# A 1 KB strip at the end of the last store, spread unevenly over the transfer engines

One Trainium2 chip, one core. The metric is the time of one execution in device microseconds; each kernel was run several times, and all runs compared here are of the fast state (a single run counts as of unknown state and is marked).

## The reference

The kernel turns 32 x 3 images of 256 x 256 float32 by 180 degrees. Seen flat, each image is reversed.

```python
def reference(x):                       # x: (32, 3, 256, 256) float32
    return np.rot90(x, k=2, axes=(-2, -1)).astype(np.float32)
```

## The kernel before

The 96 images are taken in three groups of 32. One image lies on four partitions, a quarter of it (E = 16384 elements, 64 KB) on each, so one group fills a tile of 128 partitions. VectorE reverses each row inside the tile in pieces; the store writes the four quarters of an image in reverse order. All transfers are issued by the sync engine.

```python
    G = 32
    E = L // 4                       # 16384 elements, 64 KB per partition
    ...
    def load(t, g, lo=0, hi=E):
        nc.sync.dma_start(out=t[:, lo:hi], in_=x4[g][:, lo:hi])

    def store(t, g):
        nc.sync.dma_start(out=o4[g][:, ::-1, :], in_=t[:, :])
    ...
    load(A, 0, 0, N)                 # N = E // 32
    load(A, 0, N, E)
    load(Bt, 1)
    load(Ct, 2)
    for g, t in enumerate((A, Bt, Ct)):
        inside(t)                    # 12 VectorE copies reverse each row
        store(t, g)
```

## Time and profile before

| | before |
|---|---|
| time, median of 3 runs (range) | 123.1 us (123.06 to 123.44) |
| span of the profiled run | 121.1 us |
| packet time, share of 16 engines | 97.4% |
| VectorE busy | 36% |

The time is that of a whole execution; the span runs from the first to the last instruction of one profiled execution. The page's main lines stand in the prediction below. One more, from the timeline of before (start, length, engine, line, operation), shows when the sync engine has nothing more to issue:

```profile
76.33 1.23 DVE L53 COPY Ct<-T 128x2048 f32<-128x2048 f32 x1
77.59 0.54 SPq L59 DMA_DIRECT2D out_dram<-Ct  x1
```

The last copy ends at 77.6 us and the last store is issued at once. The other 43.5 us are transfers draining, then the close of the program.

Three kinds of record in the trace are finer than the page, and the argument rests on them: each transfer engine's **packets** (start, length, size), the **landings** (the times at which a transfer's completion mark of one engine arrives at its semaphore, 16 for a transfer over 16 engines) and the sync engine's **waits** at the end. Numbers in ns below come from these records.

### The profile page before, as it was taken

The numbers are of one execution on the slowest core, as the hardware profiler recorded it, in microseconds if no ns is written. First come the engines' busy times: TensorE is split into PE (matmuls) and PEld (weight loads), VectorE is DVE, ScalarE is ACT, GpSimd is POOL, SyncE is SP. The second block draws the span as 40 slices with busy tenths as digits, with TensorE's granted clock in tenths as the row PEclk, the third lists the DMA queues.
The fourth block names the chain that finished last, engine by engine and source line by source line (L and its number), as shares of the span: only waits on it lengthen the run. The fifth ranks groups of instructions, "written<-read, shape, count | busy, mean of one in ns | idle before, by whom it ended". The sixth has DMA issues, their size and how long they took to land.

```text
span 121.1 us, 94 instructions
## 1 busy us (share of the span) xinstructions
DVE 44.2 (36%) x36; POOL 0.2 (0%) x4
## 2 busy tenths in 40 slices
DVE  0000000599994199998039999600000000000000
POOL 0000000000000000000000000000000000000000
DMA  9977987897799879978989977997799779977980
GB/s 359 399 336 336 650 356 336 346 693 346 346 411 628 346 346 476 563 346 346 346 346 476 563 346 346 563 476 346 346 584 455 346 346 606 433 346 346 671 368 0
DMA packets 1008, 50.33 MB, mean 416 GB/s; under 512 B 112, under 2 KB 112, under 8 KB 240
## 3 DMA queue, kind: packets, MB, share of 16 engines
q1 hardware_dynamic: 1008, 50.33, 97.4%
HBM read 25.17 MB, written 25.17 MB: 416 GB/s over the span
## 4 chain that ended last, share of the span: by engine, by line
DMA 33%; DVE 25%; another core or an unknown queue 4%; issue 1%; SPq 1%; DVEq 0%
DMA Bt<-in_x_dram 33%; DVE T L53 8%; DVE Ct L53 8%; DVE Bt L53 8%; SPq L56 1%; DVEq L53 0%
## 5 line engine op out<-in xcount | busy, mean ns | idle before, releaser
L53 DVE COPY T<-A 128x2048 f32<-128x2048 f32 x4 | 4.9, 1227 | 22.7 <-DMA A<-in_x_dram 22.6
L53 DVE COPY T<-Ct 128x2048 f32<-128x2048 f32 x4 | 4.9, 1227 | 5.4 <-DMA Ct<-in_x_dram 5.3
L53 DVE COPY T<-Bt 128x2048 f32<-128x2048 f32 x4 | 4.9, 1227 | 4.4 <-DMA Bt<-in_x_dram 4.3
L53 DVE COPY Bt<-T 128x2048 f32<-128x2048 f32 x4 | 4.9, 1227 | 0.1
L53 DVE COPY A<-T 128x2048 f32<-128x2048 f32 x4 | 4.9, 1227 | 0.1
L53 DVE COPY Ct<-Ct 128x2048 f32<-128x2048 f32 x4 | 4.9, 1227 | 0.1
L53 DVE COPY Bt<-Bt 128x2048 f32<-128x2048 f32 x4 | 4.9, 1227 | 0.1
L53 DVE COPY A<-A 128x2048 f32<-128x2048 f32 x4 | 4.9, 1227 | 0.1
L53 DVE COPY Ct<-T 128x2048 f32<-128x2048 f32 x4 | 4.9, 1227 | 0.1
L89 POOL MEMSET const-bfloat16-1.0<- 128x1 bf16 x1 | 0.1, 101 | 0.0
L89 POOL MEMSET const-uint8-127<- 128x1 uint8 x1 | 0.1, 101 | 0.0
L89 POOL MEMSET const-float32-0.0<- 128x1 f32 x1 | 0.1, 98 | 0.2 <-issue 0.2
L89 POOL MEMSET const-float32-1.0<- 128x1 f32 x1 | 0.1, 98 | 0.0
## 6 DMA issues: line engine op xcount, KB each, us to landing
A<-in_x_dram SPq DMA_DIRECT2D x1, 7936.0 KB, 21.4
A<-in_x_dram SPq DMA_DIRECT2D x1, 256.0 KB, 2.8
Bt<-in_x_dram SPq DMA_DIRECT2D x1, 40.3
Ct<-in_x_dram SPq DMA_DIRECT2D x1, 60.3
out_dram<-A SPq DMA_DIRECT2D x1, 43.9
out_dram<-Bt SPq DMA_DIRECT2D x1, 43.8
out_dram<-Ct SPq DMA_DIRECT2D x1, 42.7
```

The lines of the kernel that those rows point to most:

```text
L53: tc.keep_in_program_order(nc.vector.tensor_copy(out=dst, in_=src))
L56: nc.sync.dma_start(out=t[:, lo:hi], in_=x4[g][:, lo:hi])
L89: nc = _bacc.Bacc("TRN2", target_bir_lowering=False, num_devices=1)
```

## The change

The intent is to even out the ends of the sixteen transfer engines, which do not finish the last store together. The store is cut 1 KB short on every row, and the strip that is left goes out in four transfers whose shapes put more rows on low-numbered engines and none on 14 and 15.

```diff
+    M = E // 64
-    def store(t, g):
-        nc.sync.dma_start(out=o4[g][:, ::-1, :], in_=t[:, :])
+    def store(t, g, lo=0, hi=E, i=0, j=G):
+        nc.sync.dma_start(out=o4[g][i:j, ::-1, lo:hi], in_=t[4 * i:4 * j, lo:hi])
 ...
-    for g, t in enumerate((A, Bt, Ct)):
-        inside(t)
-        store(t, g)
+    inside(A)
+    store(A, 0)
+    inside(Bt)
+    store(Bt, 1)
+    inside(Ct)
+    store(Ct, 2, 0, E - M)
+    store(Ct, 2, E - M, E, 0, 14)
+    store(Ct, 2, E - M, E, 14, 16)
+    store(Ct, 2, E - M, E, 16, 24)
+    store(Ct, 2, E - M, E, 24, 32)
```

## The prediction

> **What bounds the kernel now.** I read the head of the page first, to see whether an engine or the transfers fill the span.
>
> ```profile
> span 121.1 us, 94 instructions
> DVE 44.2 (36%) x36; POOL 0.2 (0%) x4
> ...
> DMA packets 1008, 50.33 MB, mean 416 GB/s; under 512 B 112, under 2 KB 112, under 8 KB 240
> ## 3 DMA queue, kind: packets, MB, share of 16 engines
> q1 hardware_dynamic: 1008, 50.33, 97.4%
> ```
>
> VectorE works for 36% of the span; packets fill 97.4% of what sixteen transfer engines have. So this is a kernel of transfers, and only two things shorten it: less packet time on the engine that ends last, or a shorter tail behind it. The 112 packets under 512 B are no data: 7 transfers times 16 engines, one 4-byte semaphore packet each.
>
> The chain of waits stops at 77.6 us, when the last store is issued, so I take the end from the sync queue's own waits and from the list of issues.
>
> ```profile
> SPq L100 <- DMA out_dram<-Bt: 19.3, 1, 19.3
> SPq L100 <- DMA out_dram<-Ct: 19.3, 1, 19.3
> SPq L100 <- DMA out_dram<-A: 3.5, 1, 3.5
> ...
> out_dram<-A SPq DMA_DIRECT2D x1, 43.9
> out_dram<-Bt SPq DMA_DIRECT2D x1, 43.8
> out_dram<-Ct SPq DMA_DIRECT2D x1, 42.7
> ```
>
> At the end the sync engine waits for store A, then 19.3 us more for Bt's, then 19.3 us more for Ct's. Each store takes some 43 us to land although its own packets need 19.3 us, because it queues behind older transfers. From 77.6 us the rings are therefore always full, and whatever the sync engine issues in the microseconds after that is hidden. Windows show how abruptly it ends (columns: stretch and length, VectorE busy, GpSimd busy, clock, DMA share, GB/s):
>
> ```profile
> 112.00:119.40 7.40, 0.00 (x0) 0.00 (x0) 1.00 0.98 425
> 119.40:120.00 0.60, 0.00 (x0) 0.00 (x0) 1.00 0.01 0
> 120.00:121.10 1.10, 0.00 (x0) 0.00 (x0) 1.00 0.00 0
> ```
>
> No data packet starts after 119.4 us; behind it are the semaphore packets, the landing and the close.
>
> The packet records in the trace give the rest, in us from the start of the span. The sixteen engines end their last data packet between 119.431 and 119.970: sorted, at 0, 75, 118, 172, 186, 223, 312, 313, 314, 328, 347, 398, 419, 429, 440 and 539 ns after the first. The landings on the last store's semaphore lie between 119.783 and 120.313, the same pattern some 0.34 us later. In the instruction records the sync engine's last wait starts at 120.330, the next instruction at 120.397, and the span ends at 121.103: 0.79 us from the last landing, spent on barriers. The strip goes for the uneven end. If all engines ended at their mean, offset 288 ns, the gain would be 539 - 288 = 251 ns, 0.2% of 123.1. That is the most that any such balancing can bring.
>
> **What the Trainium skill says.** "DMA: Bandwidth & Descriptors", section "Why a DMA increments its semaphore by 16 and not by 1": the number of engines is the largest k up to 16 that divides the slowest dimension of both sides, and these are the lowest-numbered k. Groups of 14, 2, 8 and 8 with four rows each therefore go to engines 0 to 13, 0 and 1, 0 to 7 and 0 to 7, four rows per engine, as the title says. The trace before agrees for k = 16 (16 landings per transfer); its records do not name the engine, so it has nothing on which engine ends when. Section "Queues, rings and completion order": each engine consumes its ring in order. The trace agrees: packets follow each other without a gap, across transfers too, a 4-byte packet costing 6 ns between them. Section "Why small descriptors are slow (HBM only)": a fixed overhead of about 3 cycles per packet. In the trace 2048 B packets start every 80 ns and 65536 B packets every 2414 ns, so a packet costs 4.7 ns plus 0.03676 ns per byte: a small overhead indeed. Section "Latency and other measured facts": engines 7 and 15 are usually the slower ones. No record here can show it.
>
> **The change part by part.** All loads, all copies, the stores of A and Bt: unchanged. The order of instructions shows one thing only, four more issues on the sync engine behind the last store.
>
> Issues: four at about 0.54 us (what the last store's issue took) are 2.2 us, from 78.1 to 80.3, some 39 us before they are needed. Path cost 0.
>
> Base of the last store: 8 packets per engine shrink from 65536 to 64512 B, 8 x 1024 x 0.03676 = 301 ns less on each engine.
>
> Strip: a 1 KB packet should cost 4.7 + 37.6 = 42.4 ns, an estimate from the two sizes above. Engines 0 and 1: 16 x 42.4 = 678. Engines 2 to 7: 12 x 42.4 = 509. Engines 8 to 13: 4 x 42.4 = 170. Engines 14 and 15: none. Semaphore packets at 6 ns add 24, 18, 6 and 0. Against before, each kind of engine ends by
>
> - 0 and 1: -301 + 678 + 24 = +401 ns
> - 2 to 7: -301 + 509 + 18 = +226 ns
> - 8 to 13: -301 + 170 + 6 = -125 ns
> - 14 and 15: -301 ns
>
> Now lay these on the sixteen offsets. The kindest assignment is that engines end in order of their number, as the change supposes. Then 0 and 1 come to 401 and 476, 2 to 7 to 344, 398, 412, 449, 538 and 539, the others to at most 304. The latest is 539, just what it was: the strip moves 701 ns between the ends of the row, where only 539 ns were to be evened out, and engines 6 and 7 become the last. Gain 0. If finishing order has nothing to do with the number, drawing the assignment at random 20,000 times makes the latest 257 ns later on average, 401 at worst.
>
> The close: the built program waits at its end for pairs of semaphores. Before, the last store's was in the last wait, and the others had long been met. After, eight semaphores serve eleven transfers, and the fourth strip's sits in the second of the four waits, the base's and third strip's in the third, the first two strips' in the last. Engines 0 to 7, which end last, carry the fourth strip; so its landing releases the second wait, and two more waits have to be stepped through. From the records a satisfied wait takes 67 ns to the next instruction (120.330 to 120.397): 2 x 67 = +134 ns.
>
> Sum: 0 + 134 = +0.13 us with order by number, 257 + 134 = +0.39 us without order. The first moments of the trace speak for a mixture. The first packets of the sixteen engines start one after the other within 0.52 us, about the 0.43 us which that issue takes, so order by number exists at the very start; but the earliest had first packets of about 600 ns and later ones of 81 ns, which scrambles it. I give order 45%, no order 55%: 0.45 x 0.13 + 0.55 x 0.39 = +0.27. I add nothing for the measurement: 123.10 + 0.27 = 123.37, and I say 123.4.
>
> **The rivals.** First, the change does what it is meant to: late engines relieved, up to 0.25 us gained, less 0.13 for the waits, so 122.9 to 123.0. It needs an ordered end with a wider spread than this one execution shows, or 1 KB packets cheaper than 42 ns; neither is in the records. Second, small writes cost more than their bytes: before has no packet of 1 KB and none under 64 KB on the store side, and the 80 ns come from reads of HBM. Were 1 KB writes to cost 80 ns, the engines with 16 rows would lose 16 x 38 = 0.6 us more and those with 12 rows 0.45: 123.8 to 124.2. Against it speaks that ring order lets the next packet start without waiting for a write's receipt; nothing shows it for writes of this size. Third, all is hidden or drowned: a change of 0.1 us against runs of before that lie between 123.06 and 123.44. That would read 123.1 to 123.2, and is what order by number nearly gives. Fourth, a wait before issue: the strips reuse the loads' semaphores, and a missing completion could hold back an issue. The built program has no wait on them, as all four loads were awaited before.
>
> **Range and chances.** The low end is order by number with a quick run, 122.95; the high end is no order, with strip packets at some 60 ns (12 to 16 rows x 18 ns = 0.2 to 0.3 us): 123.5 + 0.3 = 123.8. A change of 2% is 2.5 us; the strip's whole packet time on the most loaded engine is 0.7 us, so it would take an effect that I have no trace of. Faster by over 2%: the bound of 0.25 us excludes it but for an error of mine, 0.005. Slower: 0.015. Within: 0.98.
>
> **What would show it.** Packets: 128 of 64512 B about 2377 ns apart, 128 of 1024 B about 42 ns apart, 14 + 2 + 8 + 8 = 32 more semaphore packets: 1008 + 128 + 32 = 1168 in all. The page: DMA share still about 97%, VectorE unchanged, four more issues that end near 80.3 us. The last two waits of the sync engine some 67 ns apart and both behind the last landing. Engines that carry 12 or 16 rows should be the last; the spread of the last data packets should be as large as before or larger. Wrong would be: 1 KB packets at 60 ns or more (second rival), a spread well under 0.5 us (first rival), or a gap before the strip's packets, which would mean that the new transfers are not ready in the ring in time.

## The result

The changed kernel took 123.13 us (median of 6 runs, 123.06 to 123.57), before 123.06 (6 runs, 122.72 to 123.44). The ratio is 1.0013, with a 95% interval of 0.999 to 1.0037. Ratios here are the mean time of one kernel's runs over that of the other's of the same rounds, so not quite the ratio of the medians. So: the same within 2%, inside the predicted range of 122.95 to 123.8, and 0.27 us below the predicted 123.4. A second measurement (the run "again" below) gave 1.0012, 1.0000 to 1.0025. The first interval contains 1 and the second touches it, so the times by themselves do not settle that the change costs anything; what follows on its parts comes from single traces.

From the head of the page of the changed kernel:

```profile
span 121.4 us, 98 instructions
DVE 44.2 (36%) x36; POOL 0.2 (0%) x4
...
DMA packets 1168, 50.33 MB, mean 415 GB/s; under 512 B 144, under 2 KB 272, under 8 KB 400
...
q1 hardware_dynamic: 1168, 50.33, 97.2%
```

VectorE is untouched, and there are 1168 packets as counted: 128 strip packets and 32 completion marks more. The timeline of the changed kernel shows the five issues in one piece:

```profile
76.41 1.23 DVE L56 COPY Ct<-T 128x2048 f32<-128x2048 f32 x1
77.67 3.90 SPq L62 DMA_DIRECT2D out_dram<-Ct  x5
```

They end at 81.6 us (predicted 80.3: a strip's issue takes 0.72 to 0.95 us, not the store's 0.54). That costs nothing, as the engines do not reach the strip before 119 us. The sync queue's own waits and the windows of the end, both of the changed kernel:

```profile
SPq L110 <- DMA out_dram<-Ct: 38.6, 1, 38.6
...
SPq L110 <- DMA out_dram<-A: 0.2, 1, 0.2
```

```profile
112.00:119.40 7.40, 0.00 (x0) 0.00 (x0) 1.00 0.94 406
119.40:120.00 0.60, 0.00 (x0) 0.00 (x0) 1.00 0.48 159
120.00:121.40 1.40, 0.00 (x0) 0.00 (x0) 1.00 0.00 1
```

The wait for the store of Bt has gone from the list: the second of the closing waits now holds the last strip's semaphore too, so one wait of 38.6 us lies where two of 19.3 us were. The windows count a packet whole in the stretch in which it starts. So the 0.01 that before has from 119.4 to 120.0 us is not an idle stretch: its last 64 KB packets started by 117.6 us and ran until 119.97. By the packet records 8.8 of the sixteen engines were busy there on average in before and 9.4 in the changed kernel, 7.5 of them with strip packets. The 0.48 shows only that most strip packets start there.

The following table takes the end apart for every kernel that was run, in us for the first two columns and the span and in ns for the others. "Even end" is where the latest engine would have ended its data with 64 KB packets on all rows (its last base packet plus 0.03676 ns for each byte cut from its eight packets; 301 ns for a 1 KB strip). So even end to last packet is what the strip did to the packets within one execution, free of what differed earlier. "Landing" is from the last completion packet to the last landing, "waits" from there to the instruction behind the last closing wait, "rest" from there to the end of the span.

| kernel | even end | last data packet | landing | waits | rest | span |
|---|---|---|---|---|---|---|
| before | 119.970 | 119.970 | 338 | 84 | 706 | 121.10 |
| same (before again) | 119.971 | 119.971 | 344 | 84 | 706 | 121.11 |
| after | 120.032 | 120.061 | 363 | 194 | 733 | 121.36 |
| again (after) | 120.159 | 120.189 | 335 | 194 | 729 | 121.45 |
| oneload | 120.118 | 120.197 | 360 | 126 | 734 | 121.42 |
| half | 120.089 | 119.976 | 660 | 189 | 728 | 121.56 |
| tilt8 | 119.809 | 121.988 | 319 | 195 | 728 | 123.24 |
| uniform | 120.143 | 120.187 | 341 | 84 | 728 | 121.35 |
| sixloads | 120.361 | 120.361 | 315 | 258 | 728 | 121.67 |
| ladder | 120.154 | 120.557 | 458 | 216 | 733 | 121.97 |
| eight | 120.072 | 120.115 | 371 | 84 | 729 | 121.31 |
| bars4 | 120.083 | 120.258 | 596 | 195 | 727 | 121.78 |
| pieces | 120.103 | 120.463 | 351 | 263 | 728 | 121.81 |
| two | 120.060 | 119.979 | 336 | 84 | 728 | 121.13 |

After against before: 62 ns that were there before the strip began (even end), 29 from the strip's packets, 25 in landing, 110 in waits, 27 in the rest, in sum the 0.25 us between the two spans.

### The profile page after: what moved, and what is told of

Same layout as the page of the kernel before. It is cut to its first block, busy times and chain, and to the rows that moved or that the text cites. A ratio compares the mean times of both kernels' runs of the same rounds, so it can differ in the third digit from the quotient of the medians.

```text
span 121.4 us, 98 instructions
## 1 busy us (share of the span) xinstructions
DVE 44.2 (36%) x36; POOL 0.2 (0%) x4
## 2 busy tenths in 40 slices
DMA packets 1168, 50.33 MB, mean 415 GB/s; under 512 B 144, under 2 KB 272, under 8 KB 400
## 3 DMA queue, kind: packets, MB, share of 16 engines
q1 hardware_dynamic: 1168, 50.33, 97.2%
## 4 chain that ended last, share of the span: by engine, by line
DMA 33%; DVE 24%; another core or an unknown queue 4%; issue 1%; SPq 1%; DVEq 0%
DMA Bt<-in_x_dram 33%; DVE T L56 8%; DVE Ct L56 8%; DVE Bt L56 8%; SPq L59 1%; DVEq L56 0%
## 6 DMA issues: line engine op xcount, KB each, us to landing
out_dram<-Ct SPq DMA_DIRECT2D x1, 8064.0 KB, 42.4
```

## The experiments

**Theory.** Nothing is gained at the engines: they do end roughly in the order of their number, but the strip moves more than there is to even out. And the close is longer because the last strip's semaphore sits in the second of four waits. **Rivals:** the order of the ends is chance; engines share one limit, so unevenness does not matter; the waits cost nothing; small writes cost more than their bytes. There were twelve runs (bars4, pieces, two and same on another chip than the rest of the twelve).

### again: the change a second time

```diff
(no edit to the changed kernel)
```

> The changed kernel once more, for a second trace and a narrower interval. My theory (two more wait steps at the end cost 134 ns, uneven strip costs some 30 ns because the order of the ends follows the engine number in part): 0.1 to 0.2 us slower than before, ratio 1.001 to 1.0015; from the last landing to the end of the span 0.927 us again, against 0.790 in before; engines without strip among the late ones again. Rival (the order of the ends is drawn anew in each execution): the classes stand in another order, and the strip costs up to 0.4 us in this trace.

Measured: 123.13 us, ratio 1.0012 (1.0000 to 1.0025); close from the last landing 194 + 729 = 923 ns. To which class an engine belongs can be worked out in this trace and in all with an uneven strip, since the number of packets after an engine's last base packet gives its class (16, 12, 4 or 0); I matched the packets to the sixteen base ends with these periods, to 0.3 to 0.6 ns per packet on average. In the order in which the engines ended their base packets, the classes were

```
after    12 16 12  4 12 12  4 12 16  4 12  4  4  0  4  0
again    12 12 12 12 16 16  4 12  4  4  4 12  4  4  0  0
oneload  12 12 12 12 16 16 12 12  4  4  4  4  0  4  4  0
half     12 12 12 12 12  4 16 16  4 12  4  0  4  4  4  0
tilt8    12 12 12 16 16 12  4 12  4 12  4  4  4  0  4  0
```

Engines 14 or 15 (class 0) are last in all five, engines 2 to 7 (class 12) first in all five, and the rank correlation with the number is 0.67 to 0.82. The order differs from run to run, but not at random: the rival falls. (No record names an engine. The match shows that the transfers' sets of engines lie inside each other; that these are the lowest numbers is taken from the Trainium skill, as in the prediction.) Engines 0 and 1, which the change loads most, are not the first; they stand between second and ninth.

### tilt8: eight times the unevenness

```diff
-    M = E // 64
+    M = E // 8
```

> The same unevenness with an 8 KB strip in place of 1 KB: base 2409 ns shorter per engine, 16, 12, 4 and 0 strip packets of about 306 ns. Theory (each engine moves its own bytes at its own fixed rate, nobody else takes over): engines 0 and 1 end 2.5 us later than with even work, the kernel is 2.1 to 2.7 us slower than before, 125.2 to 125.8 us, ratio 1.017 to 1.022. Rival (the engines share one limit, and a free engine leaves its rate to the others): within 0.4 us of before, ratio under 1.004.

Measured: 125.10 us, ratio 1.0176 (1.0161 to 1.0191). Last data packet 2.18 us after the even end. The windows of this kernel's end show who works:

```profile
117.40:119.40 2.00, 0.00 (x0) 0.00 (x0) 1.00 0.66 279
119.40:120.60 1.20, 0.00 (x0) 0.00 (x0) 1.00 0.50 212
120.60:122.00 1.40, 0.00 (x0) 0.00 (x0) 1.00 0.13 53
122.00:123.20 1.20, 0.00 (x0) 0.00 (x0) 1.00 0.00 0
```

By the packets that start there, a DMA share of 0.50 is eight engines of sixteen, 0.13 is two. The packet records say it more exactly: all 128 strip packets of 8 KB take the same 309 ns and follow each other every 306 ns, early, when most engines work, and at the end, when two do. That is 26.8 GB/s for an engine, no more than with all sixteen at work (64 KB every 2414 ns, 27.1). Whoever is free takes over nothing. The shared limit falls, and the unevenness acts with the size that was computed.

### half: half the unevenness

```diff
-    M = E // 64
+    M = E // 128
```

> A 512 B strip in place of 1 KB, all else as in the change: half the unevenness. With the order of classes that the trace of the changed kernel shows, the last data packet ends some 150 ns earlier than with even work, and the two added wait steps take 134 ns back: as before within 0.1 us, ratio 0.999 to 1.001. Rival (the waits cost nothing): ratio 0.998 to 0.9995. Rival (packets of 512 B cost more than 4.7 ns plus their bytes): period over 30 ns in place of 24, and slower than before.

Measured: 123.25 us, ratio 1.0022 (1.0009 to 1.0035): slower than I expected; the interval only just touches the upper end of what I wrote (1.001). The data packets did as they should: periods of 23.5 ns, the last one 113 ns before the even end. But the last landing came 660 ns behind the last completion packet, in place of 338. So something costs time that the packet records do not show. Two later runs, bars4 and pieces, are about this.

### uniform: the strip in one transfer

```diff
-    store(Ct, 2, E - M, E, 0, 14)
-    ...                             # all four strips
+    store(Ct, 2, E - M, E)
```

> The 1 KB strip in one transfer over all sixteen engines, 8 packets each: no unevenness, and eight transfers in all, so the last landing is met by the last wait. Theory: 8 x 4.7 + 6 = 44 ns of packets more, close 0.790 us as in before: ratio 1.0003 (0.999 to 1.0015). Rival (the extra transfer as such costs, however it is spread): close longer than 0.80 us or a gap ahead of the strip's packets.

Measured: 122.90 us, ratio 0.9996 (0.9982 to 1.0010). The packets cost 44 ns to the nanosecond, landing and waits are those of before, 341 and 84 ns. So an eighth transfer as such is nearly free. The rest is 728 in place of 706 ns; see sixloads.

### sixloads: no strip, but the semaphores moved on

```diff
-    load(Ct, 2)
+    for lo, hi in ((0, 2048), (2048, 4096), ..., (8192, 10240), (10240, E)):
+        load(Ct, 2, lo, hi)
```

(applied to the kernel before)

> The kernel before, without any strip, with the load of Ct in six transfers: twelve transfers take turns on eight semaphores, and the last store's falls into the first of the four closing waits. Theory of the waits: three more steps behind the last landing, 3 x 67 = 201 ns, close 0.99 us in place of 0.79; packets 5 x (8 x 4.7 + 6) = 218 ns more; together 0.42 us slower, ratio 1.0034. Rival (the longer close of the changed kernel comes from its strips and not from the place of the wait): close 0.79 us, ratio 1.002.

Measured close: 258 + 728 = 986 ns against 790, as the theory of the waits had it (0.99). The sync queue's own waits show that the first of the closing waits held everything, from the issue of the last store to its landing:

```profile
SPq L101 <- DMA out_dram<-Ct: 42.2, 1, 42.2
```

So the place of the last store's semaphore among the closing waits sets this, and not the strips. A rest of 727 to 734 ns comes with every kernel that uses eight semaphores in place of seven, strip or not; of it, the instruction on GpSimd that clears them takes 92 ns in place of 74.

The time was a miss: ratio 1.0000 (0.9984 to 1.0015) where I expected 1.0034. The trace shows two things that met. Where the engines turn from loads to stores, the last load packet of each takes longer than its bytes: in before 1.13 us longer, mean of sixteen (3.2 to 3.8 us for 64 KB). With 24 KB packets at that place it was 0.31 us. That gives back some 0.8 us on most engines, against the 0.22 us of added packets. In the profiled run one engine was 0.77 us behind all others at the end (its landing at 120.681 us, the next at 119.907) and took the gain with it; that run was also the slowest of the four, 123.45 against 122.94 to 123.00. What the gain is worth by itself stays open.

### oneload: one wait step in place of two

```diff
-    load(A, 0, 0, N)
-    load(A, 0, N, E)
+    load(A, 0)
```

(applied to the changed kernel)

> The changed kernel with A loaded in one transfer: the semaphores move on by one, and the last strip's falls into the third of the four closing waits in place of the second. Theory of the waits: one step behind the last landing, close 0.790 + 0.067 = 0.857 us. Rival (the close does not depend on the place of the wait): 0.927 us as in the changed kernel, or 0.790.

Measured (one run, state unknown): close 126 + 734 = 860 ns. The sync queue waited twice for Ct, 19.0 us for the base and 0.3 for the last strip, one wait later than in the changed kernel:

```profile
SPq L109 <- DMA out_dram<-Bt: 19.8, 1, 19.8
SPq L109 <- DMA out_dram<-Ct: 19.3, 2, 19.0
```

With the other rows of the table the waits stand at 84 ns for no step behind the last landing, 126 for one, 189 to 216 for two (216 in ladder alone), 258 to 263 for three. The theory of the waits holds; in the change two steps cost 110 ns.

### ladder: which engine ends when

```diff
+    store(Ct, 2, 0, E - 2 * M)
+    for lo, cuts in ((E - 2 * M, (0, 15, 28, 32)), (E - M, (0, 11, 20, 27, 32))):
+        for i, j in zip(cuts, cuts[1:]):
+            store(Ct, 2, lo, lo + M, i, j)
```

(in place of the five stores of Ct)

> Two 1 KB strips cut into transfers over 15, 13, 4 and 11, 9, 7, 5 engines, four packets per engine in each: the number of packets after the base tells which engine it was, in eight classes (0 to 3 with 28 packets, 4 with 24, 5 and 6 with 20, 7 and 8 with 16, 9 and 10 with 12, 11 and 12 with 8, 13 and 14 with 4, 15 with none). Theory: low numbers among the early ends, high ones among the late, not strictly; engine 15 among the last four. Rival (no order by number): classes scattered, rank correlation near 0. Packets put the latest of engines 0 to 3 625 ns later than with even work, so some 0.4 us slower in data end, plus two wait steps.

Measured (one run, state unknown): 123.76 us; last data packet 403 ns after the even end (0.4 expected). The order of the base ends, from first to last, was: 7 or 8; 5 or 6; one of 0 to 3; 5 or 6; one of 0 to 3; 4; 13 or 14; 7 or 8; one of 0 to 3; 9 or 10; 11 or 12; one of 0 to 3; 11 or 12; 13 or 14; 9 or 10; 15. The rank correlation with the number is 0.55, and engine 15 was the last. So there is order, with wide scatter below the top. Landing took 458 ns: a hidden cost again, with seven strips. The spacing found in bars4 below explains only some 20 ns of it (178 against 175 for each of seven transfers). The latest landings of the last five strips stood 183 to 197 ns apart here; why more than in bars4 stays open.

### eight: an attempt that was built otherwise than meant

```diff
+    store(Ct, 2, 0, E - 96)
+    nc.sync.dma_start(
+        out=o4[2].rearrange("(a b) s e -> a b s e", a=8)[:, :, ::-1, E - 96:],
+        in_=Ct[:, E - 96:])
```

(in place of the five stores of Ct)

> A try at a version that beats both: a 384 B strip in a single transfer over engines 0 to 7 alone, 16 packets each, none on 8 to 15. Eight transfers in all, so no added wait step. Per engine: 8 to 15 end 113 ns earlier, 0 to 7 113 + 81 = 194 ns less 113 + ... in sum 81 + 113 - 0 = 194 ns later. With the order of classes of the changed kernel's trace the last data packet ends 629 - 113 = 516 ns (against 334 + 194 = 528) after the first base: 0.1 us earlier than before, close 0.790: ratio 0.9992. Rival (order by number not kept between executions): ratio 1.000 to 1.002.

The sum in that text is muddled; it means that engines 0 to 7 end -113 + 16 x 18.8 + 6 = 194 ns later. It came to nothing anyway: the transfer has 16 landings and not 8, presumably because the two outer dimensions, 8 and 4, were folded into 32 when it was built. What ran was an even strip of 384 B. 123.11 us, ratio 1.0024 (0.9990 to 1.0057, with one run at 124.16): inconclusive on the question. Its trace is of use still: eight packets of 384 B in one transfer, and the landing took only 371 ns.

### bars4: what delays the landing

```diff
-    store(Ct, 2, E - M, E, 0, 14)
-    ...                             # all four strips
+    for lo in range(E - M, E, M // 4):
+        store(Ct, 2, lo, lo + M // 4)
```

> Four even strips of 256 B, each over all sixteen engines, 8 packets of some 14 ns each. It asks why the last landing of the half strip came 660 ns after its last semaphore packet, 340 in before. Theory M (the completion marks of one engine land at least some 200 ns apart, which the packet records do not show): a transfer takes 119 ns of packets, so 4 x 81 = 324 ns of lag on top of 340: 0.6 to 0.7 us. Theory P (each packet of a small write takes at least some 48 ns to land): 32 x 34 = 1.09 us on top, 1.4 us. Theory U (lag comes of the unevenness or of transfers over fewer than sixteen engines): 0.34 us. Two more wait steps, 110 ns. Wall by M: 4 x 119 - 301 = 175 of packets, 324 of lag, 110 of waits, 0.6 us slower, ratio 1.005; by P 1.011; by U 1.0023.

Measured: 123.50 us, ratio 1.0033 (1.0003 to 1.0063); landing 596 ns. The latest landing of each of the five transfers came at 120.138, 120.328, 120.506, 120.684 and 120.859 us, so 190, 178, 178 and 175 ns apart, while the packets of one such transfer take 119. Nothing is uneven here and all sixteen engines take part, so theory U falls; P asked for 1.4 us. M holds, with about 178 ns in place of my 200: here an engine's completion marks arrived no closer than that. In half a strip transfer of four 512 B packets takes 100 ns of packets, four times 78 too little, which makes 312 of the 320 ns that were missing. In the change itself a transfer takes 175 ns, just about this spacing, so the delay there is small: 335 to 363 ns against 338 and 344.

### pieces: many small packets, few marks

```diff
+    R = E - 8 * M
+    store(Ct, 2, 0, R)
+    for s in (1, 2, 3):
+        nc.sync.dma_start(out=o4[2][:, 3 - s, R:], in_=Ct[s::4, R:])
+    for odd in (0, 64):              # row 0 of each group, 256 B pieces
+        nc.sync.dma_start(
+            out=o4[2][:, 3, R:].rearrange("g (j e) -> g j e", e=128)[:, :, odd:odd + 64],
+            in_=Ct[0::4, R:].rearrange("p (j e) -> p j e", e=128)[:, :, odd:odd + 64])
```

(in place of the five stores of Ct)

> The last 8 KB of each row of Ct in five transfers: rows 1 to 3 of each group in 8 KB packets, row 0 in two transfers of 256 B pieces, 32 packets per engine in each, all sixteen engines, no unevenness. Packets: -2409 + 3 x (2 x 306 + 6) + 2 x (32 x 14.1 + 6) = 359 ns more. Three more wait steps, 174 ns. Theory M (completion marks at least 200 ns apart): every transfer takes over 450 ns, so no lag is added: 0.34 us from last semaphore packet to last landing, 0.53 us slower, ratio 1.0043. Theory P (each small packet takes at least 48 ns to land): 64 x 34 = 2.2 us of lag on top, ratio 1.022.

Measured: 123.61 us, ratio 1.0042 (1.0016 to 1.0068), 1.0043 expected. Last data packet 360 ns after the even end (359 expected), landing 351 ns after 64 packets of 256 B per engine. Down to 256 B the writes cost their bytes and 4.7 ns each, and no more; theory P falls, and with it my second rival.

### two: strips without added waits

```diff
-    store(Ct, 2, E - M, E, 0, 14)
-    ...                             # all four strips
+    store(Ct, 2, E - M, E, 0, 24)
+    store(Ct, 2, E - M, E, 24, 32)
```

> A try at a version that keeps what the traces support: the 1 KB strip in two transfers, 24 groups over engines 0 to 11 (8 packets each) and 8 groups over engines 0 to 7 (4 more). Nine transfers in all, so the last strip is met by the last wait and no step is added. Against before engines 0 to 7 end 220 ns later, 8 to 11 44 ns later, 12 to 15 301 ns earlier. Theory (engines 14 and 15 among the last, as in every trace so far): last data packet some 50 ns earlier than with even work, some 25 ns of lag added, close as in before: ratio 0.9995 to 1.0005, faster than the change by 0.1 us. Rival (two strips cost as four do): ratio 1.0013.

Measured: 123.03 us, ratio 0.9998 (0.9974 to 1.0022). In the trace the eight engines of class 12, 0 to 7, were the first eight, one of 12 to 15 was last, and the last data packet came 81 ns before the even end; waits and landing as before. That is the one kernel in which what the packets gain reaches the last landing (half gained 113 ns of packets and lost 322 in landing), and the eighth semaphore takes 22 of the 81 ns back. Some 60 ns are 0.05% and cannot be seen in the times. It is no worse than before and no better that could be shown.

### same: before once more

```diff
(no edit to the kernel before)
```

> The kernel before, unchanged: a second trace of it, to see what varies by itself. Theory: the last landing 0.34 us behind the last semaphore packet, 84 ns from the last landing to the instruction after the last wait, both as in the first trace; the end of the last data packet between 119.8 and 120.2 us, as far apart as the other traces put their starting point; the rest of the close 0.71 to 0.73 us. Ratio 1.000 within 0.0015.

Measured: 122.91 us, ratio 0.9991 (0.9964 to 1.0018). Even end 119.971 us, landing 344, waits 84, rest 706: the first trace to within 6 ns. Even ends over all traces with a strip lie between 119.81 and 120.16 us, which is set before the strip begins, so two spans from single traces are not to be compared to 0.1 us.

## Why the prediction was right, point by point

- **Bound and hidden issues.** Right. Packets fill 97.2% of the engines' time, the issues end at 81.6 us, and no gap precedes the strip's packets. So the fourth rival, a wait before issue, did not come (in ladder it did: its last strip was issued at 101.2 us, when the store of Bt had landed, still early enough). The windows were over-read: the end is not as abrupt as I wrote, see above.
- **Packet costs.** Right. Strip packets start 42 to 43 ns apart (42.4 estimated), and uniform (44 ns) and pieces (360 ns) confirm the sum on either side of 1 KB.
- **The strip moves more than there is to even out.** Right. In the three traces with the change's own strip the last data packet came 29, 30 and 79 ns after the even end, so 46 ns on average; never before it. Its details were off: the last were not engines 6 and 7 but class 16, engines 0 or 1, in all three. The signs that I had named came: the last five engines are of class 12 or 16 in each, and the spread of the last data packets (627, 512 and 477 ns) is about that of the same trace's base ends (629, 484 and 486). (By the listed terms the strip moves 702 ns, not 701.)
- **Order by number, 45 to 55.** This is the mis-sized term. I put 0.55 x 257 = 141 ns on having no order at all; with the order that every trace shows it was 46. (Of the signs of order, the first issue took 0.39 us, not 0.43.) Engines 14 and 15 are late often enough that relieving them works, and the loss is only that 0 and 1 were not early enough for sixteen rows.
- **Close.** Right in sum, and that is luck: 134 ns predicted, 137 measured between the two traces, but two steps are 110 ns, and the other 27 come from the eighth semaphore, which I had not counted. The place of the wait as the cause was right (sixloads, oneload).
- **Sum.** 46 + 110 + 25 for the eighth semaphore + some 12 of landing = 0.19 us, where I had 0.27. The two measurements give 0.0013 x 123.06 = 0.16 and 0.0012 x 122.94 = 0.15 us. The agreement is no proof: the intervals of these ratios are wider than any of the terms, and no change at all would have lain in my range too.
- **Rivals.** That it is drowned in the spread (third rival, 123.1 to 123.2) describes the number best. Cheap relief (first) did not come. Dear small writes (second) do not exist in the form I gave, but dear small transfers do: the completion marks. At 1 KB and four packets per engine the change passes just beside that limit.

The Trainium skill, "DMA: Bandwidth & Descriptors", section "Why a DMA increments its semaphore by 16 and not by 1", held for the number of engines: the strips' semaphores got 14, 2, 8 and 8 landings at the end, besides one entry each when the strip was issued. That the lowest-numbered engines are taken no run here shows; the match of packets to classes shows only that the same engines are taken first each time.

## What to carry to other kernels

Before evening out the ends of parallel engines, read the spread of their ends from the trace: it bounds the gain (0.25 us of 123 here), and the correction must be smaller than the spread. Then count what the extra transfers add behind the last byte: the place of their semaphores among the closing waits, some 40 to 70 ns per step here, and the spacing of each engine's completion marks, some 180 ns here. In these runs few transfers with many packets did better than many with few (pieces against bars4: landing 351 and 596 ns).

## What the Trainium skill lacked or had wrong

- "DMA: Bandwidth & Descriptors": no page gives a least spacing of one engine's completion marks. Here it is about 178 ns (bars4: 175 to 190 ns between latest landings, with 119 ns of packets per transfer; 183 to 197 in ladder), and it is not visible in the packet records.
- The same page, "Latency and other measured facts", calls engines 7 and 15 usually the slower ones, but ties this to transfers that GpSimd issues, so it says nothing on these, which the sync engine issues; no page says in which order the engines end. In seven traces that tell classes apart the latest base end was always among those without strip packets (14 and 15 in five, 15 in one, 12 to 15 in one). It was late by its start, not by its rate: in before all packets after 62.5 us take the same time, and the 539 ns between the engines stand already when the stores begin, at 61.5 to 62.0 us.
- The same page, "Why small descriptors are slow (HBM only)", gives about 3 cycles per packet, at 32 B a cycle. Measured 4.7 ns per packet, at 256 B, 1 KB, 2 KB and 64 KB alike; with 0.03676 ns per byte a cycle of 32 B is 1.18 ns, so this is about 4 cycles (an estimate from the page's 32 B).
- No page has the cost of turning from loads to stores: the last load packet of each engine took 1.13 us longer than its bytes (before), and 0.31 us with 24 KB packets at that place (sixloads). A smaller last load might be worth more than all that was tried here; it was not run by itself.
- No page has the cost of the closing waits: 84, 126, 189 to 216 and 258 to 263 ns for none to three steps behind the last landing, and 21 to 28 ns more for eight semaphores in place of seven.
